# Where the modulation pieces of the second layer are computed: in the FFNs, or all of them inside the Even mixer

## The chip, the cores and the metric

One core of one Trainium2 chip runs the whole program. The metric is the device time of one execution in microseconds; less is better. Engines are named as the profile names them: PE is TensorE's matmul stream, PEld its weight loads, DVE is VectorE, ACT is ScalarE, POOL is GpSimd, SP is SyncE, which here only issues DMAs.

## What is computed

Two trunk layers over 640 tokens, 128 of context and 512 latent ones, with 1024 features. A layer is a half-step FFN, a mixer and a second half-step FFN, each between a modulated norm and a gated norm. The mixer of the first layer (Even) is a gated DeltaNet beside a latent attention (MLA); that of the second (Odd) is a gated linear attention. The nine modulation vectors of a layer come from one small product per layer:

```python
def adaln(cond, w, b):
    m = (jax.nn.silu(cond) @ w + b).reshape(cond.shape[0], 1, N_MOD, D_MODEL)
    return [m[:, :, j] for j in range(N_MOD)]
...
for i in range(DEPTH):
    m_ctx = adaln(c_ctx[None, :], mod_w[i], mod_b[i])
    m_lat = adaln(c, mod_w[i], mod_b[i])
    xc = ffn_branch(xc, m_ctx[0:3], ...)
    ...
    yc, s_ctx = odd_mixer(hc, *w, s0)
    ...
    xs = xs + m_lat[5] * rmsnorm(ys, norm_post[i, 1])
```

`mod_w[i]` is 1024 x 9216, so its bytes are many and its rows of `cond` are two (context and latent). The product depends on nothing else that the layers compute and may be done at any time before its use.

## The kernel before

The order of the work is that of the layers: first FFN, Even mixer, second FFN (both of layer 0), third FFN, Odd mixer, fourth FFN (layer 1). All matmuls of the layers are made of three products of high and low parts (L208 the projections, L650 the up matmuls of the FFNs, L298 the down and out projections). An FFN is a loop over column tiles of L650, with L298 for two token groups (384 and 256 tokens).

**The modulation.** `adaln` (L364 to L421) is a generator. Each step of it is a piece: one of eight row blocks (128 rows) of one of five column groups of a layer; groups 0 to 3 have 2048 columns, group 4 has 1024. There are 80 pieces. A piece loads two tiles `mw` of 512 KB (one in group 4) on SP's queue (L376), into the pool of load buffers of which there are seven, which the weights of the FFNs and of the out projection use too. While the Even mixer's code runs (`look` is true) the next piece's load is issued one piece ahead. At each second piece the matmuls L395 of the pair are issued: for either row block one product per column tile of 512 columns, four tiles (two in group 4), with the 32 columns of `cT` as the stationary side; the four column tiles lie side by side in the array (`tile_position`) and accumulate in one PSUM bank `ad`, of which there is one. The profile shows each such product as two records, so a pair is 16 records, 8 in group 4. After the last row block a bias tile `mb`, taken from the load buffers as well, is loaded on ACT's queue, added by DVE (L403), for groups 0 to 3 turned by four transposes on PE (L407) into a bank of the PSUM pool `pt`, and copied out (L413), or multiplied and written as gates (L415 to L420). In the mixer the banks of `pt` are held by its ring of work banks (`misc`), until the mixer's end.

**Who asks for pieces.** Whoever calls the filler: eight pieces before the first FFN; the FFNs, `FILLS[layer][n]` = (pieces in the loop, pieces at its tail); the Even mixer with `self.fill(n)` in its projections, its heads, its MLA heads (`MFILL`) and beside; the Odd mixer with a flush. The first FFN takes 22, so pieces 1 to 30 are out when the mixer starts. The mixer asks for 31, up to piece 61, the second FFN for 16, and the third for the three left.

**The Even mixer's gated DeltaNet.** Its four heads and two directions are worked as two pairs of heads. For a pair come, in this order: `gdn_prep` (L1164; the decay matrices of five chunks: transposes and products on PE, then DVE and ACT), `gdn_inverse` (L1191; DVE alone, row by row), `gdn_levels` (L1226; two levels of products L1232, L1236 and transposes L1239 on PE with copies on ACT and DVE between them, then a last one), and `gdn_chain`, which walks the state through `gdn_step` (L1259) in five steps. The second pair's work and the MLA's (L1488 to L1584) are written so that one lies beside the other.

**What sets the order.** A tile scheduler orders each engine's instructions when the program is built: by the order of the code, raised for marked parts, and by what is ready and which buffers are free. The engines then run their rows strictly in that order.

Of the kernel before, what the change touches and what calls it, by code (L numbers as in the profile page):

```python
# [27 lines left out]
HW = (6400, 4096)  # L28
HT = TOK // 2
PLAIN = 2  # L30
FILLS = (((16, 6), (10, 6)), ((18, 0), (0, 0)))
EARLY = 5
SLOTS = ((2, 3, 4, 5, 6), (0, 1, 2, 3, 4))
TW = 648
# [858 lines left out]
class Even(Mixer):  # L893
# [87 lines left out]
    def run(self, nxt):  # L981
# [184 lines left out]
        def gdn_prep(pair, st, misc, ering):  # L1166
            for c in range(NT):
                cs = slice(c * P, (c + 1) * P)
                pb, pk, E = misc(), misc(), ering()
                for u, d, h in units(pair):  # L1170
                    nc.tensor.transpose(un(pb, u), gc[:, d, c, h:h + 1].to_broadcast([P, P]), T.ident)
                for h2 in range(2):
                    kc = k[2 * pair + h2][:, cs]
                    nc.tensor.matmul(un(pk, 2 * h2), lhsT=kc, rhs=kc, start=True, stop=True)
                    nc.tensor.matmul(un(pk, 2 * h2 + 1), lhsT=kc, rhs=q[2 * pair + h2][:, cs], start=True, stop=True)
                for u, d, h in units(pair):
                    nc.vector.scalar_tensor_tensor(un(E, u), un(pb, u), gc[:, d, c, h:h + 1], neg[d], ALU.subtract, ALU.min)
                nc.scalar.activation(E[:, :512], E[:, :512], AF.Exp)
                pair_view = lambda t, h2: t[:, h2 * 256:h2 * 256 + 256].rearrange("p (d t) -> p d t", d=2)
                if c:  # L1180
                    Qe = st.Q[c]
                    nc.scalar.activation(Qe, pb, AF.Exp)
                    for h2 in range(2):
                        w = pair_view(Qe, h2)
                        nc.vector.tensor_mul(w, w, q[2 * pair + h2][:, cs].unsqueeze(1).to_broadcast([P, 2, P]))
                for h2 in range(2):
                    nc.vector.tensor_mul(pair_view(st.att[c], h2), pair_view(E, h2), un(pk, 2 * h2 + 1).unsqueeze(1).to_broadcast([P, 2, P]))
                for u, d, h in units(pair):
                    nc.vector.scalar_tensor_tensor(un(st.A[c], u), un(pk, 2 * (u // 2)), nbp[:, c, d * 4 + h:d * 4 + h + 1], un(E, u), ALU.mult, ALU.mult)
# [35 lines left out]
        def gdn_levels(st):  # L1225
            for lv in (4, 5):  # L1226
                mask = T.cm[:, lv].unsqueeze(1).to_broadcast([P, 4, P])
                for c in range(NT):
                    a, uu, dd = st.A[c], st.U[c], st.D[c]
                    py, pz = misc(), misc()  # L1230
                    for u in range(4):
                        nc.tensor.matmul(un(py, u), lhsT=un(a, u), rhs=un(dd, u), start=True, stop=True)  # L1232
                    Y = ering()
                    nc.scalar.copy(Y[:, :512], py)
                    for u in range(4):
                        nc.tensor.matmul(un(pz, u), lhsT=un(Y, u), rhs=un(uu, u), start=True, stop=True)  # L1236
                    nc.vector.copy_predicated(v4(uu), mask, v4(pz))
                    for u in range(4):
                        nc.tensor.transpose(un(py, u), un(uu, u), T.ident)  # L1239
                    nc.scalar.copy(dd, py)  # L1240

            lo, hi = slice(0, 64), slice(64, 128)
            where = ((hi, lo), (lo, hi))
            for c in range(NT):
                a, uu, dd = st.A[c], st.U[c], st.D[c]
                py, pz, Y = misc(), misc(), ering()
                for u in range(4):
                    r, k = where[u % 2]
                    nc.tensor.matmul(un(py, u)[r, k], lhsT=un(a, u)[:, r], rhs=un(dd, u)[:, k], start=True, stop=True, tile_position=(0, r.start))
                by = lambda t, d: t[:, :512].rearrange("p (h d t) -> p h d t", h=2, d=2)[:, :, d]  # L1250
                for d, (r, k) in enumerate(where):
                    nc.scalar.copy(by(Y, d)[r, :, k], by(py, d)[r, :, k])
                for u in range(4):
                    r, k = where[u % 2]
                    nc.tensor.matmul(un(pz, u)[k, r], lhsT=un(Y, u)[:, k], rhs=un(uu, u)[:, r], start=True, stop=True, tile_position=(0, k.start))
                for d, (r, k) in enumerate(where):
                    nc.vector.tensor_copy(by(uu, d)[k, :, r], by(pz, d)[k, :, r])

        def gdn_step(pair, st, work, S, cu, last, ctx):  # L1259

            at = lambda c: slice(c * P, (c + 1) * P)
            if not last:
                pt, kdt = misc(), work()
# [23 lines left out]
            for u, d, h in units(pair):  # L1287
                c = cu[d]
# [10 lines left out]
        def gdn_chain(pair, st):  # L1299
# [19 lines left out]
            def context():  # L1319
                po = gdn_step(pair, st, work, S0, (0, 0), False, True)  # L1320
                for u, d, h in units(pair):
                    nc.scalar.dma_start(self.outs["new_gdn_state"][0, 0, d, h], un(S0, u))
                    od = oT[h][:, 0:P]
                    if d == 0:
                        nc.scalar.copy(od, un(po, u))
                    else:
                        nc.vector.tensor_add(od, od, un(po, u))
                        square(h, 0)
# [64 lines left out]
        self.mark = T.tc.tile_snap_priority()  # L1393
        st0 = gdn_store(0)
        gdn_prep(0, st0, misc, ering)
        gdn_inverse(0, st0, ering)
        for b in range(4):
# [26 lines left out]
        def mla_keys():  # L1424
# [41 lines left out]
            nc.scalar.dma_start(self.outs["new_mla_ckv"][0, 0], nck)  # L1466
        mla_keys()
        gdn_levels(st0)
        gdn_chain(0, st0)
        st1 = gdn_store(1)  # L1470
        e1 = Ring([T.W(name="E") for _ in range(2)])
        gdn_prep(1, st1, mb, e1)


# [134 lines left out]
        gdn_inverse(1, st1, ering)  # L1609
        early = [gdn_out(0)]  # L1610
        gdn_levels(st1)
        self.fill(2)
        gdn_chain(1, st1)
# [417 lines left out]
def trunk_kernel(tc, i, cst, outs):  # L2031
    nc = tc.nc
    with ExitStack() as ctx:
# [11 lines left out]
        for l in range(2):  # L2045
            for n in range(3):
                a = (mods(l, n), gates(l, n), step)
                if n != 1:
                    subs.append(Ffn(T, i["ffn_w_in"][l, n // 2], i["ffn_w_out"][l, n // 2], *a, FILLS[l][n // 2]))
                elif l == 0:  # L2050
# [41 lines left out]
```

## Time and profile before

| | |
|---|---|
| time, median of 3 runs | 2714.06 us (2709.87 to 2714.55) |
| profiled execution | 2716.26 us, span 2714.5 us |
| PE busy | 2632.5 us, 97% of the span, 16040 records |
| PEld busy | 2331.2 us, 86% |
| DVE busy | 1943.0 us, 72% |
| ACT busy | 1179.1 us, 43% |
| POOL busy | 125.5 us, 5% |
| read from and written to memory | 286.59 MB and 20.33 MB |

The span is what lies between the first and the last instruction of the profiled execution. Busy times of an engine are the union of its records; matmuls overlap, so a record may be longer than the time to the next one. In the views by stage, PEclk is the granted TensorE clock as a share of full speed. In a timeline a row is a group of records of one line, its first number the start of the first of them, and in brackets stands the idle time ahead of it and what ended it.

### The profile page before, as it was taken

The numbers are of one execution on the slowest core, as the hardware profiler recorded it, in microseconds if no ns is written. First come the engines' busy times: TensorE is split into PE (matmuls) and PEld (weight loads), VectorE is DVE, ScalarE is ACT, GpSimd is POOL, SyncE is SP. The second block draws the span as 40 slices with busy tenths as digits, with TensorE's granted clock in tenths as the row PEclk, the third lists the DMA queues.
The fourth block names the chain that finished last, engine by engine and source line by source line (L and its number), as shares of the span: only waits on it lengthen the run. The fifth ranks groups of instructions, "written<-read, shape, count | busy, mean of one in ns | idle before, by whom it ended". The sixth has DMA issues, their size and how long they took to land. (4 is left out here: it accounts for less than half of the span.)

```text
span 2714.5 us, 41232 instructions
## 1 busy us (share of the span) xinstructions
PE 2632.5 (97%) x16040; PEld 2331.2 (86%) x16040; DVE 1943.0 (72%) x3731; ACT 1179.1 (43%) x2281; POOL 125.5 (5%) x301
## 2 busy tenths in 40 slices
PE   6999999999999999999999999999999999999998
PEld 4988888789858678888997999999899988999997
DVE  5777777768585558777778777777675749777776
ACT  5433333554345645332335433334765447333333
POOL 0000000200100010000001000000200002000001
PEclk8999999999999999999999999999999999999999
DMA  8334424734151334343227322224212143332222
GB/s 272 123 115 141 148 96 133 251 103 142 50 188 46 128 117 130 114 138 103 86 71 244 104 87 86 86 81 135 92 55 67 59 140 109 95 92 86 78 70 101
DMA packets 297099, 309.60 MB, mean 114 GB/s; under 512 B 13573, under 2 KB 250639, under 8 KB 296903
## 3 DMA queue, kind: packets, MB, share of 16 engines
q1 hardware_dynamic: 278240, 260.05, 30.1%
q10 hardware_dynamic: 18663, 46.92, 4.9%
q8 instruction: 126, 2.06, 0.3%
q14 instruction: 70, 0.57, 0.1%
HBM read 286.59 MB, written 20.33 MB: 113 GB/s over the span
## 5 line engine op out<-in xcount | busy, mean ns | idle before, releaser
L650 PE MATMUL up<-ar,hi 128*128 128x320 f32 x2944 | 658.6, 311 | 10.5 <-ACT ar L513 4.5
L650 PEld LDWEIGHTS up<-ar,hi 128*128 128x128 f32 x2944 | 502.4, 189 | 37.2 <-ACT ar L513 6.1
L650 PE MATMUL up<-ar,lo 128*128 128x320 f32 x1472 | 455.5, 310 | 0.6 <-DVE lo L604 0.6
L603 ACT CAST hi<-raw 128x1024 fp32r<-128x1024 f32 x256 | 268.1, 1050 | 295.4 <-PE up L650 258.4
L304 DVE TENSOR_TENSOR y<-y,dn 128x512 f32<-128x512 f32 x388 | 264.5, 682 | 151.9 <-PE dn L298 150.8
L604 DVE TENSOR_TENSOR lo<-raw,hi 128x1024 fp32r<-128x1024 f32 x256 | 312.4, 1222 | 75.1 <-ACT hi L603 74.5
L298 PE MATMUL dn<-hi,al 128*128 128x512 f32 x880 | 347.8, 395 | 0.1
L298 PE MATMUL dn<-lo,ah 128*128 128x512 f32 x880 | 347.6, 395 | 0.0
L298 PE MATMUL dn<-hi,ah 128*128 128x512 f32 x880 | 346.8, 395 | 0.7 <-DVE y L304 0.5
L650 PE MATMUL up<-hq,hi 128*128 128x320 f32 x1408 | 315.1, 310 | 0.3 <-DVE xn L707 0.3
L650 PEld LDWEIGHTS up<-ar,lo 128*128 128x128 f32 x1472 | 277.9, 189 | 1.3 <-DVE lo L604 1.3
L208 PE MATMUL up<-ar,hi 128*128 128x384 f32 (+1 forms) x1184 | 267.3, 315 | 4.9 <-ACT ar L274 4.0
L650 PEld LDWEIGHTS up<-hq,hi 128*128 128x128 f32 x1408 | 238.8, 188 | 21.5 <-issue 9.2
L650 PE MATMUL up<-hq,lo 128*128 128x320 f32 x704 | 217.4, 309 | 0.0
L208 PEld LDWEIGHTS up<-ar,hi 128*128 128x128 f32 x1184 | 200.6, 191 | 15.3 <-issue 5.6
L183 DVE TENSOR_TENSOR lo<-raw,hi 128x1024 fp32r<-128x1024 f32 x145 | 175.8, 1218 | 45.0 <-ACT hi L182 38.2
L298 PEld LDWEIGHTS dn<-hi,al 128*128 128x128 f32 x880 | 165.3, 188 | 39.3 <-DVE al L691 1.2
L298 PEld LDWEIGHTS dn<-hi,ah 128*128 128x128 f32 x880 | 165.2, 188 | 26.3 <-DVE y L304 1.4
L208 PE MATMUL up<-ar,lo 128*128 128x384 f32 (+1 forms) x592 | 184.3, 311 | 0.0
L298 PEld LDWEIGHTS dn<-lo,ah 128*128 128x128 f32 x880 | 165.1, 188 | 22.2
L182 ACT CAST hi<-raw 128x1024 fp32r<-128x1024 f32 x145 | 150.9, 1048 | 44.5 <-PE up L208 19.0
L658 ACT COPY h<-up 128x320 f32<-128x320 f32 x68 | 29.0, 426 | 314.3 <-PE up L650 314.3
(704 smaller groups left out, 4216.2 us busy)
## 6 DMA issues: line engine op xcount, KB each, us to landing
raw<-in_ffn_w_in_dram SPq DMA_DIRECT2D x188, 512.0 KB
mw<-in_mod_w_dram SPq DMA_DIRECT2D x144, 512.0 KB
raw<-in_ffn_w_out_dram SPq DMA_DIRECT2D x88, 512.0 KB
xdr<-x ACTq DMA_DIRECT2D x25, 512.0 KB
x<-xdr ACTq DMA_DIRECT2D x25, 512.0 KB
raw<-in_od_w_in_dram SPq DMA_DIRECT2D x24, 512.0 KB
raw<-in_ev_w_in_dram SPq DMA_DIRECT2D x19, 512.0 KB
gb<-gate ACTq DMA_DIRECT2D x12, 512.0 KB
```

Of the source, the lines that this page charges most:

```text
L182: nc.scalar.copy(hi, raw)
L183: nc.vector.tensor_sub(lo, raw, hi.bitcast(F32))
L208: self.nc.tensor.matmul(ps[:, :n], lhsT=wt[a][:, kc], rhs=self.h[g][:, b, kc], start=k == 0, stop=k == 3 * KC - 1)
L298: nc.tensor.matmul(ps, lhsT=a(i, m), rhs=w[j][:, nh * 512:nh * 512 + 512], start=k == 0, stop=k == last)
L304: nc.vector.tensor_add(yd, yd, ps)
L603: nc.scalar.copy(hi, raw[:, :n])
L604: nc.vector.tensor_sub(lo, raw[:, :n], hi.bitcast(F32))
L650: nc.tensor.matmul(ps[:, :HT], lhsT=w[i][:, kc], rhs=b[j].at(kc), start=first and n == 0, stop=n == 11, skip_group_check=not first)
L658: self.T.nc.scalar.copy(p1, X[:, :HT])
```

## The change

The second and third FFN ask for no pieces any more. In their place the Even mixer asks for up to 23 more: one in each of the five chunks of the second pair's `gdn_prep`, one at each odd chunk of the two levels of `gdn_levels` (four a call, two calls), and one at the start of each `gdn_step` (five a chain, two chains). The mixer now asks for more than the 50 pieces that are left, and the last of them is given out before its end.

```diff
@@ -28,7 +28,7 @@
 HW = (6400, 4096)
 HT = TOK // 2
 PLAIN = 2
-FILLS = (((16, 6), (10, 6)), ((18, 0), (0, 0)))
+FILLS = (((16, 6), (0, 0)), ((0, 0), (0, 0)))
 EARLY = 5
 SLOTS = ((2, 3, 4, 5, 6), (0, 1, 2, 3, 4))
 TW = 648
@@ -1167,6 +1167,8 @@
             for c in range(NT):
                 cs = slice(c * P, (c + 1) * P)
                 pb, pk, E = misc(), misc(), ering()
+                if pair:
+                    self.fill(1)
                 for u, d, h in units(pair):
                     nc.tensor.transpose(un(pb, u), gc[:, d, c, h:h + 1].to_broadcast([P, P]), T.ident)
                 for h2 in range(2):
@@ -1228,6 +1230,8 @@
                 for c in range(NT):
                     a, uu, dd = st.A[c], st.U[c], st.D[c]
                     py, pz = misc(), misc()
+                    if c % 2:
+                        self.fill(1)
                     for u in range(4):
                         nc.tensor.matmul(un(py, u), lhsT=un(a, u), rhs=un(dd, u), start=True, stop=True)
                     Y = ering()
@@ -1258,6 +1262,7 @@
 
         def gdn_step(pair, st, work, S, cu, last, ctx):
 
+            self.fill(1)
             at = lambda c: slice(c * P, (c + 1) * P)
             if not last:
                 pt, kdt = misc(), work()
```

The line numbers of the code behind the second and third hunk shift: L1232, L1236 and L1239 of before are L1236, L1240 and L1243 in the changed kernel, and the MLA's lines are five higher.

Three places of PE's order show what moves. In these rows `ad` is the pieces' PSUM bank, `mw` their weight tile (a number for each), `x2` two products alike.

The first place is the end of the second FFN (L298, its down projection; L257, the transposes of the next norm) and the start of the third (L650). Before:

```order
6066 L298 MATMUL dn_13681<-lo_13272,ah_13247 128x512
6067 L298 MATMUL dn_13681<-hi_13271,al_13248 128x512
6068 L257 MATMUL pt_13622<-ident,xn_13603 128x128 x4
6069 L395 MATMUL ad_10645<-mw_13695,cT 32x512
6070 L395 MATMUL ad_10645<-mw_13697,cT 32x512 x2
6071 L650 MATMUL up_13862<-ar_13346,hi_13495 128x320
6072 L650 MATMUL up_13888<-ar_13346,hi_13501 128x320
6073 L650 MATMUL up_13862<-ar_13346,hi_13495 128x320
6074 L650 MATMUL up_13862<-ar_13346,lo_13496 128x320
6075 L407 MATMUL pt_13710<-ident,mb_13707 128x128 x4
6076 L395 MATMUL ad_13719<-mw_13720,cT 32x512 x2
```

After:

```order
6088 L298 MATMUL dn_13745<-lo_13336,ah_13311 128x512
6089 L257 MATMUL pt_13669<-ident,xn_13667 128x128 x4
6090 L298 MATMUL dn_13745<-hi_13335,al_13312 128x512
6091 L257 MATMUL pt_13686<-ident,xn_13667 128x128 x4
6092 L650 MATMUL up_13883<-ar_13410,hi_13559 128x320
6093 L650 MATMUL up_13909<-ar_13410,hi_13565 128x320
6094 L650 MATMUL up_13883<-ar_13410,hi_13559 128x320
```

The pieces' products and the transposes of the bias tile (L407) are gone from here, and the up matmuls follow the transposes directly.

The second place is in `gdn_levels` of the second pair (`ar` and `E` are its matrices, `pt` and `dn` the work banks). Before:

```order
3286 L1236 MATMUL dn_4818<-ar_7144,E_5415 128x128 x4
3287 L1236 MATMUL pt_4820<-ar_7144,E_5416 128x128 x4
3288 L1532 MATMUL up_6648<-ckv_6424,ukv_7259 128x384
3289 L1239 MATMUL pt_4821<-ident,ar_7144 128x128 x4
3290 L1532 MATMUL up_6646<-ckv_6424,ukv_7259 128x384
3291 L1239 MATMUL dn_4819<-ident,ar_7144 128x128 x4
3292 L1232 MATMUL pt_4821<-ar_7145,ar_7144 128x128 x4
3293 L1232 MATMUL dn_4819<-ar_7145,ar_7144 128x128 x4
3294 L1236 MATMUL dn_4818<-ar_7144,E_5415 128x128 x4
```

After:

```order
3317 L395 MATMUL ad_7900<-mw_8026,cT 32x512
3318 L1236 MATMUL pt_4821<-ar_7226,ar_7225 128x128 x4
3319 L1236 MATMUL dn_4819<-ar_7226,ar_7225 128x128 x4
3320 L395 MATMUL ad_7900<-mw_8026,cT 32x512
3321 L395 MATMUL ad_7900<-mw_8028,cT 32x512 x2
3322 L395 MATMUL ad_7900<-mw_8128,cT 32x512
3323 L1240 MATMUL dn_4818<-ar_7225,E_5415 128x128 x4
3324 L1240 MATMUL pt_4820<-ar_7225,E_5416 128x128 x4
3325 L1243 MATMUL pt_4821<-ident,ar_7225 128x128 x4
3326 L395 MATMUL ad_7900<-mw_8128,cT 32x512
3327 L395 MATMUL ad_7900<-mw_8130,cT 32x512 x2
```

Two groups of four matmuls used to follow each other, or one of the MLA's stood between them; now products of the pieces do, one to four at a time. Over the whole mixer the products of the second layer's pieces stand in 29 runs before, 80 products in all, and in 54 runs after, 136 products.

The third place is the mixer's end (L298 the out projection, the others the last MLA head). Before:

```order
3635 L1575 MATMUL dn_4818<-ident,pr_8481 128x128
3636 L298 MATMUL dn_8881<-ar_8203,oh_7728 128x512 x2
3637 L407 MATMUL pt_7479<-ident,mb_7476 128x128 x4
3638 L407 MATMUL pt_8374<-ident,mb_8371 128x128 x4
3639 L1579 MATMUL up_6646<-V_7261,cq_6425 128x128
3640 L1579 MATMUL up_6646<-V_7262,cq_6425 128x128 x2
```

After:

```order
3675 L1580 MATMUL dn_4818<-ident,pr_8656 128x128
3676 L298 MATMUL dn_9036<-ar_8414,oh_7869 128x512 x2
3677 L407 MATMUL pt_7011<-ident,mb_7008 128x128 x4
3678 L407 MATMUL pt_7361<-ident,mb_7358 128x128 x4
3679 L1584 MATMUL up_6646<-V_7400,cq_6425 128x128
3680 L1584 MATMUL up_6646<-V_7401,cq_6425 128x128
3681 L407 MATMUL pt_7687<-ident,mb_7684 128x128 x4
3682 L1584 MATMUL up_6646<-V_7401,cq_6425 128x128
3683 L407 MATMUL pt_8210<-ident,mb_8207 128x128 x4
```

Before, the transposes of two finished column groups stand here; now those of all four do.

## Rows read from the trace of the kernel before

**Rows 1.** Page, section 1: busy us, share of the span, instructions of each engine.

```profile
PE 2632.5 (97%) x16040; PEld 2331.2 (86%) x16040; DVE 1943.0 (72%) x3731; ACT 1179.1 (43%) x2281; POOL 125.5 (5%) x301
```

**Rows 2.** Table by stage, the second, third and fourth FFN: us, each engine's busy us (instructions), PEclk, DMA share, GB/s.

```profile
1015.60:1442.10 426.50, 421.46 (x2531) 386.24 (x2532) 323.59 (x504) 163.31 (x257) 8.72 (x15) 1.00 0.36 114
1470.90:1892.40 421.50, 420.41 (x2492) 385.22 (x2492) 319.67 (x507) 161.28 (x256) 9.16 (x21) 1.00 0.33 102
2269.00:2683.00 414.00, 409.86 (x2457) 382.33 (x2456) 317.01 (x496) 159.99 (x251) 6.69 (x12) 1.00 0.29 89
```

**Rows 3.** Table by stage, the mixer in four stretches: the inverse's, and the sum.

```profile
745.00:820.00 75.00, 71.74 (x445) 45.91 (x446) 62.17 (x290) 37.27 (x122) 2.71 (x3) 1.00 0.52 189
...
sum 275.00, PE 267.47 PEld 202.45 DVE 174.11 ACT 139.11 POOL 15.71; mean PE 66.87 PEld 50.61 DVE 43.53 ACT 34.78 POOL 3.93
```

**Rows 4.** Waits of PE, 685 to 960 us (total, times, longest): first and last of eleven.

```profile
PE up L1457 <- POOL ro L235: 1.9, 1, 1.9
...
PE dn L1236 <- ACT E L1234: 0.2, 1, 0.2
```

**Rows 5.** Timeline of PE, second FFN (start, us, line, operation, records).

```profile
1112.22 1.92 PE L395 MATMUL ad<-mw,cT 128*32 128x512 f32 x16
1114.08 0.56 PE L650 MATMUL up<-hq,hi 128*128 128x320 f32 x2
```

**Rows 6.** Timeline of PE, Even mixer.

```profile
738.81 1.07 PE L395 MATMUL ad<-mw,cT 128*32 128x512 f32 x8
739.81 0.49 PE L1271 MATMUL pt<-g,kq 128*128 128x128 f32 x2
740.23 1.04 PE L395 MATMUL ad<-mw,cT 128*32 128x512 f32 x2
741.20 0.49 PE L1271 MATMUL pt<-g,kq 128*128 128x128 f32 x2
```

**Rows 7.** Groups of PE by line: L395 in 1000 to 1600, then in 685 to 960.

```profile
L395 PE MATMUL ad<-mw,cT 128*32 128x512 f32 x112 | 20.8, 632 | 0.0
...
L395 PE MATMUL ad<-mw,cT 128*32 128x512 f32 x160 | 31.5, 604 | 0.0
```

**Rows 8.** Table by stage, the first 200 records of L650 in each FFN.

```profile
1015.60:1053.70 38.10, 32.15 (x200) 30.86 (x201) 0.96 0.42 125
1470.90:1509.60 38.70, 30.56 (x200) 29.42 (x201) 0.96 0.52 171
2269.00:2304.60 35.60, 30.57 (x200) 29.33 (x200) 1.00 0.38 119
```

**Rows 9.** Timeline of PE, from the second FFN to the third.

```profile
1458.23 1.90 PE L395 MATMUL ad<-mw,cT 128*32 128x512 f32 x10
1460.06 0.50 PE L298 MATMUL dn<-hi,ah 128*128 128x512 f32 x1
...
1467.60 1.06 PE L395 MATMUL ad<-mw,cT 128*32 128x512 f32 x6
1470.94 0.81 PE L650 MATMUL up<-ar,hi 128*128 128x320 f32 x3 [2.29 <-ACT ar L513]
...
1472.02 0.63 PE L407 MATMUL pt<-ident,mb 128*128 128x128 f32 x4
1472.58 5.32 PE L395 MATMUL ad<-mw,cT 128*32 128x512 f32 x16
1477.83 0.56 PE L650 MATMUL up<-ar,hi 128*128 128x320 f32 x2
```

**Rows 10.** Table by stage, a stretch of that place.

```profile
1473.00:1476.40 3.40, 3.40 (x10) 0.76 (x8) 3.40 (x10) 0.81 (x3) 0.00 (x0) 0.50 0.64 191
```

**Rows 11.** Transfers of 685 to 960 us: GB/s in 40 slices.

```profile
GB/s 0 2 5 86 116 0 2 38 259 310 22 261 244 4 173 285 304 127 184 76 60 0 2 0 40 0 4 38 248 49 405 8 0 2 229 271 114 77 137 245
```

**Rows 12.** Timeline of PE, the mixer's end.

```profile
948.90 1.05 PE L407 MATMUL pt<-ident,mb 128*128 128x128 f32 x8
```

**Rows 13.** Waits of SP's queue, 685 to 960 us (total, times, longest).

```profile
SPq L376 <- PE ad L395: 135.7, 17, 29.0
```

## The prediction, made before the changed kernel ran

> **What bounds the kernel now.** The page's busy times come first: TensorE (PE) is busy 97% of the span, VectorE 72%, ScalarE 43% [rows 1]. So the first question of any moved work is what PE pays for it at its new place. The table by stage comes second. The second, third and fourth FFN run the same matmuls, and only the fourth holds no modulation piece: 426.50, 421.50 and 414.00 us, with PE busy to within 5.0, 1.1 and 4.1 us of the whole [rows 2]. The stretch of the Even mixer that takes the moved pieces, 685 to 960 us, is 275.00 us long with PE busy 267.47, so PE stands still there for 7.5 us in all; even under the long VectorE inverse (745 to 820 us, VectorE busy 62.17 of 75) it is 3.3 us [rows 3]. The view of waits confirms it: the longest in that stretch is 1.9 us, the shortest of eleven 0.2 [rows 4]. Both the place that gives and the place that takes are full.
>
> **What a piece costs.** L395 is one 512-column product per row block and column tile. Two runs of it are found in the timeline. In the FFN a whole pair of row blocks (16 records) goes in one run: from 1112.22 to the next matmul at 1114.08, 1.86 us [rows 5]. In the mixer the scheduler cuts the pairs: a run of 8 records takes 738.81 to 739.81, 1.00 us; a run of 2 takes 740.23 to 741.20, 0.97 [rows 6]. The price is thus per run, not per record: the column tiles of one run go side by side, and a run with only one of them lasts as long as one with four. I take 0.98, between these two, for a run in which no column tile comes twice, 1.86 where one does.
>
> **Term 1, what leaves the FFNs.** 112 records move out, the others (160) are in the mixer already [rows 7]. In pairs that is the last of column group 2, four of group 3 and four half-wide ones of group 4.
> - Second FFN: it is 12.5 us longer than the fourth [rows 2]. Its first 200 up matmuls take 38.10 us against 35.60 [rows 8], and no piece runs in them, so 2.5 of it stay. Returned: 10.0. (Its four runs at 1.86 and one set of L407 at 0.56 [rows 9] make only 8.0, the lower bound.)
> - Third FFN: 7.5 longer [rows 2], all of it with pieces in it: a run of 16 takes 5.25 us, from 1472.58 to 1477.83 [rows 9], since PE had stood still for 2.29 us just before and then ran 3.40 us at a granted clock of 0.50, which is 1.2 of 2.4 GHz [rows 10]. I count all 7.5. If the wait stays and other matmuls run at the half clock instead, half of 3.4 is kept and 5.8 come back.
> - Between the two, a run of 10 records at 1458.23, 1.83 us [rows 9], returned. The run of 6 at 1467.60 lies ahead of the 2.29 us wait for ScalarE and covers part of it: returned 0, and 1.06 at most, if the wait doesn't grow.
> Sum 19.3, between 15.6 (8.0 + 5.8 + 1.8) and 22.9 (12.5 + 7.5 + 1.83 + 1.06).
>
> **Term 2, what the mixer pays.** The order of PE's rows is fixed when the program is built, so the runs can be counted ahead. Before, the pieces of the second layer in the mixer make 29 runs, 28 of 0.98 and one of 1.86: 29.3 us. After, they make 54, of which 51 at 0.98, two at 1.86 and one (ten products in a row, so one tile thrice) at 2.74: 56.4 us. That is 27.1 more for nine more pairs, which uncut would cost 16.7 (9 x 1.86; a half-wide pair has two column tiles and still two products in each). The cuts are seen in the second order shown above: in the second pair's levels one to four products of a pair stand between two groups of four matmuls. Two more L407 sets, 0.56 each, come to the mixer's end: 1.1. Against it stand PE's idle 7.5 us. The runs are put ahead of whatever the scheduler has ready, mostly not at the waits (which hang on VectorE and ScalarE and move along with PE's delay), so I let them absorb 2. Sum +26.2. Bounds: 10.3 (uncut and all 7.5 absorbed: 16.7 + 1.1 - 7.5), and 35.7 (nothing absorbed, and the waits twice as long because the inverse starts later and the same attention matmuls have to cover it: 27.1 + 1.1 + 7.5).
>
> **What costs nothing.** The moved loads (28 tiles of 512 KB at most) and bias loads are the same bytes, earlier. In the mixer more than a third of the slices show under 25 GB/s [rows 11], so there is room; what happens if the buffers run out is a rival below. VectorE does two more L403 adds and their copies there, while it is busy 174 of 275 us [rows 3]; PE, not VectorE, sets that pace outside the inverse. On SP's queue the loads of the attention weights, of the out projection and of the second FFN now stand behind more piece loads; none of PE's eleven waits hangs on a load now, so I take nothing for it, and the doubled waits above hold its bound. ScalarE gets two bias loads: under 1 us of queue time.
>
> **Sum.** -19.3 + 26.2 = +6.9. On the profiled execution, 2716.26 us, that is 2723.2; this execution is 2.2 above the median of the three runs shown, 2714.06, so I forecast **2721**. The least a measurement of this kernel can tell from no change is about 0.2%, 5.4 us. The bounds of both terms together give -12.6 (10.3 - 22.9) to +20.1 (35.7 - 15.6), that is 2701 to 2734.
>
> **Rival 1: cutting costs only the switch.** If the column tiles of different runs do not lose their overlap (a short run's tail lies under the neighbouring matmuls), a cut costs what two runs of 8 cost over one of 16: 2 x 1.00 - 1.86 = 0.14 us [rows 5, 6]. Then the mixer pays 16.7 + 25 x 0.14 + 1.1 - 2 = 19.3, and the time is 2714, no change. Against it: the run of 2 records kept PE for 0.97, with a plain transpose right behind it [rows 6]. Chance 0.20. The Trainium skill has a rule of this kind: TensorEngine Tiling (Array Packing), under Key Properties, says that a change of the tiling mode drains the engine, so by it alone every extra run has the same small price; the row of the short run speaks for the larger one.
>
> **Rival 2, the other sign: the new places are free.** The new steps stand where the chain of the state and the inverse leave PE waiting for VectorE and ScalarE. If the pieces go in uncut and take all of the 7.5 us, the mixer pays the lower bound, 10.3, and the time is 2714 - 9.0 = 2705. It becomes faster by more than the measurement's 5.4 once the mixer pays under 13.9, that is when over half of the 28.2 is hidden; the view shows 7.5 us to hide it in [rows 3, 4]. What speaks for it: a busy PE is not PE at its peak, and waits of a few tenths may lie inside the matmuls' modelled ends. Chance 0.12. Here too a page bears on it: the Trainium skill, Perfetto Trace Analysis, Identifying the Most-Contended Engine, calls matmul busy time a poor measure and would read the weight loads instead, which are busy 202.45 of the 275 us [rows 3]; by that, there would be 72 us of room and the pieces would be free, 2695. The runs in the timeline, each of which moves the next matmul by its whole length [rows 6], do not bear that out.
>
> **Rival 3: the load buffers run out.** A finished column group keeps its bias tile in one of the seven load buffers until its L407 has run, and L407 waits for the mixer's last steps: the L407 of both groups that end in the mixer now runs at 948.90, close to its end [rows 12]. After the change four groups end there (the third order above), so the last eight pairs load through four and then three buffers, and SP already waits 135.7 us for pieces to free them [rows 13]. If PE, which works strictly in order, meets at each of these eight pairs a tile that is not there, it pays one tile's transfer each time: 512 KB at 310 GB/s [rows 11], 1.7 us, an estimate. 8 x 1.7 = 13.6 more: 2734. For it: order and buffers. Against: each piece's load is issued one piece ahead. Chance 0.18.
>
> That the change does not do what it says can be left out: in PE's order the last piece stands inside the mixer.
>
> **How the numbers follow.** Forecast 0.50 (2715 to 2727, from halving or doubling what is absorbed and from the ends of term 1), rival 1 0.20, rival 2 0.12, rival 3 0.18. Faster by over 5.4 us (under 2709): nearly all of rival 2 and a little of rival 1, 0.13. Within: the rest of rival 1 and the lower third of the forecast, 0.35. Slower: 0.52. The range 2709 to 2733 leaves out rival 2 and half of rival 3.
>
> **What would show it.** After the change the second and third FFN should take about 416.5 and 414 us and hold no L395; the stretch of the mixer should hold 272 records in 54 runs and be 26 us longer, with PE still busy over 95% of it. A mixer only 17 to 20 longer is rival 1, one 10 to 14 longer with PE's idle time gone is rival 2, and waits of PE at L395 for loads are rival 3. I am wrong in the sign of term 2's surplus if a run of 2 records moves the next matmul by much less than 0.97 us.

## The result, and the profile after

The changed kernel takes 2741.14 us (median of 4 runs, 2737.16 to 2745.10) against 2714.31 before: a ratio of 1.0103, 95% interval 1.0084 to 1.0121. It is slower, as forecast, but by 26.8 us where 6.9 were forecast, and outside the range (2709 to 2733). The profiled execution's span grew from 2714.5 to 2739.0, by 24.5.

The page's first section of the changed kernel, beside [rows 1]:

```profile
PE 2653.9 (97%) x16040; PEld 2337.8 (85%) x16040; DVE 1940.2 (71%) x3731; ACT 1180.2 (43%) x2281; POOL 129.3 (5%) x301
```

TensorE is 21.4 us busier, with the same 16040 records. The table by stage for the second, third and fourth FFN, beside [rows 2]:

```profile
1055.80:1473.20 417.40, 412.40 (x2463) 384.55 (x2464) 318.51 (x498) 163.29 (x257) 8.73 (x15) 1.00 0.32 95
1500.90:1914.80 413.90, 412.33 (x2455) 385.60 (x2456) 315.90 (x496) 161.09 (x258) 12.19 (x21) 0.99 0.30 90
2292.90:2706.90 414.00, 409.86 (x2456) 382.10 (x2455) 317.06 (x496) 160.02 (x251) 6.71 (x12) 1.00 0.30 89
```

The second FFN is 9.1 us shorter and the third 7.6, and all three now take 414 to 417 us. With 1.1 between the two, 17.8 came back: close to the 19.3 of term 1.

The rest is the mixer. From the last up matmul of the first FFN to the first of the second, the table by stage shows before:

```profile
480.90:1015.60 534.70, 518.32 (x3384) 415.10 (x3383) 359.89 (x1072) 270.09 (x677) 45.27 (x119) 0.99 0.37 126
```

and after:

```profile
479.10:1055.80 576.70, 558.36 (x3504) 423.30 (x3503) 364.21 (x1087) 271.10 (x677) 45.41 (x119) 0.98 0.43 144
```

It grew by 42.0 us; TensorE is busy in 40.0 of them, so it waits only some 2 more (16.4 and 18.3). The stretch that answers to 685 to 960 us of before ends at 1000.2 now, 40 us longer, and TensorE is busy in 97% of it. Its table row and its group of L395, which answer to [rows 3] and [rows 7]:

```profile
685.00:1000.20 315.20, 304.96 (x1980) 208.91 (x1979) 177.13 (x628) 138.72 (x383) 15.76 (x18) 0.97 0.43 145
```

```profile
L395 PE MATMUL ad<-mw,cT 128*32 128x512 f32 x272 | 63.3, 607 | 2.5 <-DMA mw<-in_mod_w_dram 1.9 <-DVE mb L403 0.4
```

All 272 records are here, as counted. A run's time, from its start to the next matmul, adds up over the mixer to 79.7 us where it was 50.3: 29.4 more, for 27.1 forecast. Nothing in TensorE's waits takes the place of a bound (engine, line, what it waited for, total, times, longest):

```profile
PE pt L257 <- DVE xn L252: 4.6, 2, 2.8
PE pt L1276 <- DMA g<-in_state_gdn_dram: 2.5, 3, 1.2
PE ad L395 <- DMA mw<-in_mod_w_dram: 2.4, 5, 1.0
```

What the forecast did not have is in the granted clock. In the table by stage, around 951 us:

```profile
947.00:951.00 4.00, 3.17 (x13) 1.81 (x11) 3.60 (x8) 3.28 (x6) 0.00 (x0) 0.97 0.39 137
951.00:964.10 13.10, 13.10 (x37) 8.87 (x37) 5.31 (x23) 4.34 (x15) 0.00 (x0) 0.50 0.08 27
964.10:966.00 1.90, 1.90 (x14) 1.58 (x13) 0.52 (x2) 1.77 (x6) 0.00 (x0) 0.91 0.22 91
```

13.1 us at 1.2 GHz, in which TensorE is busy throughout. The timeline ahead of it (start, length, line, operation, records; in brackets the idle time ahead):

```profile
929.36 1.04 PE L395 MATMUL ad<-mw,cT 128*32 128x512 f32 x2
...
947.81 0.35 PE L1551 MATMUL up<-hq 128*128 128x256 f32 x1 [0.61 <-DVE hq L1506]
...
950.35 0.38 PE L1551 MATMUL pt<-kr,ar 128*128 128x256 f32 x1 [0.17 <-ACT ar L1528]
```

The last piece stands at 929.36; two short idle times of 0.61 and 0.17 us come just before the clock falls, in the scores of the third and fourth MLA head. Before, the same heads had pieces between their scores and kept the full clock, as a row of the timeline and the table by stage around it show:

```profile
917.83 1.06 PE L395 MATMUL ad<-mw,cT 128*32 128x512 f32 x8
...
910.00:942.00 32.00, 31.73 (x188) 22.13 (x186) 17.96 (x59) 19.74 (x56) 0.00 (x0) 1.00 0.37 133
```

### The profile page after: what moved, and what is told of

Its sections match the earlier page's. It is cut to its first block, busy times and chain, and to the rows that moved or that the text cites. A ratio compares the mean times of both kernels' runs of the same rounds, so it can differ in the third digit from the quotient of the medians.

```text
span 2739.0 us, 41272 instructions
## 1 busy us (share of the span) xinstructions
PE 2653.9 (97%) x16040; PEld 2337.8 (85%) x16040; DVE 1940.2 (71%) x3731; ACT 1180.2 (43%) x2281; POOL 129.3 (5%) x301
## 5 line engine op out<-in xcount | busy, mean ns | idle before, releaser
L650 PE MATMUL up<-ar,hi 128*128 128x320 f32 x2944 | 661.3, 312 | 12.1 <-ACT ar L513 5.8
L650 PEld LDWEIGHTS up<-ar,hi 128*128 128x128 f32 x2944 | 504.6, 190 | 36.7 <-ACT ar L513 6.7
L650 PE MATMUL up<-ar,lo 128*128 128x320 f32 x1472 | 456.7, 311 | 0.6 <-DVE lo L604 0.6
L298 PE MATMUL dn<-hi,ah 128*128 128x512 f32 x880 | 347.2, 395 | 1.0 <-DVE y L304 0.8
L298 PE MATMUL dn<-hi,al 128*128 128x512 f32 x880 | 347.9, 395 | 0.0
L298 PE MATMUL dn<-lo,ah 128*128 128x512 f32 x880 | 347.5, 395 | 0.0
L650 PE MATMUL up<-hq,hi 128*128 128x320 f32 x1408 | 314.3, 310 | 1.1 <-DVE xn L707 1.1
L650 PEld LDWEIGHTS up<-ar,lo 128*128 128x128 f32 x1472 | 279.0, 190 | 1.3 <-DVE lo L604 1.3
L650 PEld LDWEIGHTS up<-hq,hi 128*128 128x128 f32 x1408 | 239.1, 188 | 18.2 <-issue 6.7
L650 PE MATMUL up<-hq,lo 128*128 128x320 f32 x704 | 217.2, 309 | 0.0
L298 PEld LDWEIGHTS dn<-hi,al 128*128 128x128 f32 x880 | 165.3, 188 | 39.2 <-DVE al L691 0.9
L298 PEld LDWEIGHTS dn<-hi,ah 128*128 128x128 f32 x880 | 165.2, 188 | 26.6 <-DVE y L304 2.1
L298 PEld LDWEIGHTS dn<-lo,ah 128*128 128x128 f32 x880 | 165.1, 188 | 22.4
```

What stands on the lines that cost most here:

```text
L298: nc.tensor.matmul(ps, lhsT=a(i, m), rhs=w[j][:, nh * 512:nh * 512 + 512], start=k == 0, stop=k == last)
L650: nc.tensor.matmul(ps[:, :HT], lhsT=w[i][:, kc], rhs=b[j].at(kc), start=first and n == 0, stop=n == 11, skip_group_check=not first)
```

## The experiments

Every kernel's mixer (from the first FFN's last up matmul to the second's first) is taken apart in the same way: the time in runs of pieces (from each run's start to the next matmul), TensorE's idle time (length less busy time), and half of the time at a granted clock of 0.50, which is what such a stretch costs work that would go at 1.00. The rest is what is left.

| kernel | time, us | mixer | runs of pieces | idle | half of the time at 0.50 | rest |
|---|---|---|---|---|---|---|
| before | 2714.31 | 534.7 | 50.3 | 16.4 | 3.4 | 464.6 |
| changed | 2741.14 | 576.7 | 79.7 | 18.3 | 10.2 | 468.5 |
| e1 changed again | 2738.61 | 574.7 | 79.4 | 17.7 | 10.2 | 467.4 |
| e2 changed, uncut | 2737.35 | 572.6 | 62.7 | 32.8 | 17.0 | 460.1 |
| e3 before, uncut | 2720.99 | 536.2 | 42.5 | 21.3 | 13.6 | 458.8 |
| e4 without gdn_prep's pieces | 2734.24 | 570.4 | 75.6 | 18.9 | 8.5 | 467.4 |
| e5 bias early | 2734.79 | 579.1 | 80.9 | 18.8 | 11.9 | 467.5 |
| e6 uncut, bias early | 2729.52 | 570.8 | 63.7 | 33.0 | 13.6 | 460.5 |
| e7 gdn_prep first | 2752.64 | 587.4 | 82.2 | 23.0 | 18.7 | 463.5 |
| e8 before, gdn_prep first | 2727.13 | 547.2 | 51.6 | 19.5 | 18.7 | 457.4 |
| e9 before, no pieces in the MLA | 2729.96 | 532.2 | 27.4 | 24.6 | 17.0 | 463.2 |
| e10 before, bias early | 2714.55 | 537.6 | 49.1 | 15.5 | 10.2 | 462.8 |
| e11 gdn_step's pieces only | 2733.44 | 560.4 | 65.8 | 16.1 | 8.5 | 470.0 |
| e12 gdn_levels' pieces only | 2737.29 | 567.9 | 66.4 | 21.9 | 10.2 | 469.4 |
| e13 changed, clock kept | 2741.53 | 577.0 | 78.8 + 7.9 | 16.7 | 5.1 | 468.5 |
| e14 before and 23 products | 2745.26 | 562.5 | 52.6 + 22.5 | 15.3 | 6.8 | 465.3 |

(7.9 and 22.5 are the added products' times, from the timeline.) The rest stays within 457 to 470 us through all sixteen, so the other three columns carry most of the differences between the kernels; of a few microseconds the table can't tell the cause. Half of the time is also somewhat too much where TensorE waits within a stretch, as in e8 (busy 24.01 of 27.3 us).

**e1: the same again.** No edit.

> The changed kernel once more, unaltered, for the stretch in the last MLA heads in which TensorE ran 13.1 us at a granted clock of 0.50 (951 to 964 us), which costs about 6.5 us. Theory A (the clock falls there because the pieces are used up before these heads and nothing keeps TensorE fed through the waits at their start): the stretch is there again, at the same place and about as long; time about 2741 us. Rival (the clock falls by chance in single executions): no such stretch, or one elsewhere, and about 2734 us.

2738.61 us (ratio 1.0096, 1.0081 to 1.0111). The stretch is there again at the same place, 10.2 us long:

```profile
950.50:960.70 10.20, 10.20 (x30) 7.05 (x30) 4.45 (x19) 3.57 (x12) 0.00 (x0) 0.50 0.00 0
```

So it belongs to the kernel and is not an accident of one execution. Its length does vary: half of it is 5.1 us here and 6.8 in the changed kernel's profile, and e1 has another 3.4 us at 0.50 at 745.7.

**e2 and e3: pairs uncut.** In `adaln`, for the changed kernel and for the kernel before:

```diff
-for k, wt, j in [(k, wt, j) for k, wt in held for j in range(nj)] ...:
-    nc.tensor.matmul(..., start=k == 0, stop=k == KC - 1, ...)
...
+todo = [(k, wt, j) for k, wt in held for j in range(nj)] ...
+first, last = (0, KC - 1) if one else (1, KC - 2)
...
+for k, wt, j in todo if one else todo[::-1]:
+    nc.tensor.matmul(..., start=k == first, stop=k == last, ...)
```

> The changed kernel with the products of a pair issued last tile first, so that a pair can begin only when all its tiles are there and one product per column tile always stands together: in TensorE's order 62 runs of pieces in place of 83, by 0.98 us for a run and 0.87 for each further round of column tiles 79.9 us in place of 101.4. Theory (the price is per run): 21 us less, about 2720 us. Rival (a cut costs only the switch, 0.14 us each): 3 us less, about 2738 us. Second rival (the loads or the load buffers set the pace, not the runs): no change, and waits of TensorE for the tiles' loads grow.

> The kernel before with the same edit: 55 runs of pieces in place of 68, by the price per run 80.0 us in place of 92.7. Theory (price per run): 12.7 us less, about 2701 us. Rival (switch only): 2 us less, about 2712 us.

2737.35 (1.0092, 1.0077 to 1.0107) and 2720.99 us (1.0027, 1.0014 to 1.0039): no measurable gain for the one, a loss for the other, where the price per run alone had asked for 2720 and 2701. The mixer's time in runs did fall, by 17.0 and 7.8 us for 21 and 11 runs fewer, which is nearer to the price per run than to the switch's 0.14 each; idle time rose by 14.5 and 4.9 and the half clock took 6.8 and 10.2. A pair that begins with its last tile needs its tiles at once and is ready later, and so is the group's end. VectorE's timeline in e2 shows the bias load as the new wait, with the levels' own step queued right behind it:

```profile
869.53 0.69 DVE L406 TENSOR_TENSOR mb<-mb,ad 128x512 f32<-128x512 f32 x1 [8.37 <-DMA mb<-in_mod_b_dram]
870.14 0.72 DVE L1244 COPY_PREDICATED ar<-cm,dn 128x512 f32<-128x512 uint8 x1
```

and TensorE's waits show both, the tiles' loads and the levels' transposes that hang on that step:

```profile
PE ad L398 <- DMA mw<-in_mod_w_dram: 5.4, 6, 2.0
...
PE pt L1246 <- DVE ar L1244: 4.3, 1, 4.3
```

**e5 and e6: the bias early**, at the group's start and into a small buffer of its own, for the changed kernel and for e2:

```diff
+bias = self.S([P, 512], "bias", 1)
+nc.scalar.dma_start(bias[0:rows], ...)
...
-nc.scalar.dma_start(mb[0:rows, 0:512], ...)
-nc.vector.tensor_add(mb[0:rows, 0:512], mb[0:rows, 0:512], ps[0:rows, :])
+nc.vector.tensor_add(mb[0:rows, 0:512], bias[0:rows], ps[0:rows, :])
```

> The changed kernel with each column group's bias loaded at the group's start into a small buffer of its own; the load buffer is taken only when the sum is written. Theory C (TensorE's runs of pieces set the mixer's length) and theory D (the chain of the second pair's gdn_prep, inverse and levels sets it) both expect no change, 2737 to 2743 us, since VectorE waits for the bias under 2 us in the changed kernel. Rival (the bias loads and the load buffers hold the mixer up): 5 us less or more than that.

> Pairs uncut as in e2, and the bias early as in e5: takes away the 16.5 us that VectorE waited for bias loads in e2, where TensorE's time in runs had fallen by 17 us and its idle time had risen by 14.5. Theory C (price per run; e2 lost it to waits that its own edit brought): idle time of TensorE in the mixer falls from 33 to about 20 us and the time to about 2725. Theory D (the chain of the second pair sets the mixer's length, whatever TensorE's sum): levels of the second pair start near 838 us as in e2, time 2733 or more.

2734.79 (1.0080, 1.0065 to 1.0095) and 2729.52 us (1.0055, 1.0040 to 1.0070). In e5 the mixer gained nothing, 579.1 us; the few microseconds lie in the first FFN (429.5 us, 434.5 in the changed kernel). In e6 the first FFN gains the same 5 to 6, and the mixer only 1.8 against e2. Its idle time stayed at 33.0, where theory C had asked for 20, though the wait for the bias is gone; TensorE's longest waits are now spread over tile loads and several other causes, of which these are the first:

```profile
PE ad L400 <- DMA mw<-in_mod_w_dram: 7.3, 4, 4.4
PE pt L257 <- DVE xn L252: 4.6, 2, 2.8
PE pt L1362 <- DVE kq L1322: 3.4, 2, 2.5
```

So the mixer of the uncut kernel is held by waits that changed their names. Which one would be last is not settled.

**e4: without the pieces in gdn_prep.** The two lines of the diff's second hunk are left out.

> The changed kernel without the five steps in the second pair's gdn_prep: all pieces but the last pair at most still lie in the Even mixer, and they last into the third MLA head. Runs 81 in place of 83, 98.5 us of them in place of 101.4. Theory A (the clock falls where the pieces have run out): no stretch at half clock in the mixer's MLA heads, 3 us for the runs and 6.5 for the clock less, about 2731 us. Rival (the clock falls for another reason at the start of the third head, whatever the pieces do): the half clock stays, about 2738 us.

2734.24 us (1.0079, 1.0064 to 1.0094), between the two. No stretch near 951, as theory A said. But idle times of 1.3 to 2.0 us at three other places had stretches of 3.4 to 6.8 us behind them, so that the half clock cost 8.5 in place of 10.2: theory A was right on the place and wrong on the gain.

**e7 and e8: gdn_prep first.** For the changed kernel and for the kernel before:

```diff
+here = T.tc.tile_snap_priority()
 gdn_levels(st0)
 gdn_chain(0, st0)
...
-gdn_prep(1, st1, mb, e1)
+with T.ahead(T.tc.tile_snap_priority() - here):
+    gdn_prep(1, st1, mb, e1)
```

> The changed kernel with the second pair's gdn_prep given the priority of the first pair's levels, so that pieces no longer take the places that it had there before: its products stand at rows 3008 to 3059 of TensorE's order, in the changed kernel up to row 3180. The pieces make 86 runs in place of 83, 104.3 us in place of 101.4. Theory C: 3 us more, about 2742 us. Theory D (the change's price is that gdn_prep, and with it inverse and levels of the second pair, come 20 to 27 us later): the levels start near 822 us in place of 844, and the time is 10 us or more less, 2730 or under.

> The kernel before with the same priority for the second pair's gdn_prep, which there stands early already. 67 runs of pieces in place of 68, 90.9 us in place of 92.7. Theories C and D: 0 to 2 us less. If it is slower by over 3 us, the place of gdn_prep has a price of its own and e7 has to be read against that.

2752.64 (1.0138, 1.0121 to 1.0155) and 2727.13 us (1.0052, 1.0037 to 1.0067): both slower than the kernels that they were made from. The levels of the second pair did begin early in e7, at 820 us in place of 844, and the mixer was longer all the same: theory D falls as it was put on record. The run is no clean test of it, though: the last of the levels' products L1236 stands at 874.5 us, in the changed kernel at 871.3, so the chain began earlier and did not end earlier. e8 shows what the move costs by itself, and if that price adds up in e7 too, the early start gained 1.8 us of mixer (10.7 us longer in e7, 12.5 in e8) and not 10. e8's mixer is 12.5 us longer, and the half clock takes 15.3 more, nearly all in one stretch in the first MLA head, in which no piece stands:

```profile
796.60:823.90 27.30, 24.01 (x73) 16.84 (x73) 15.14 (x57) 13.26 (x45) 0.00 (x0) 0.50 0.05 18
```

**e9: no pieces in the MLA heads**, on the kernel before:

```diff
-MFILL = ((1, 1, 1, 1, 1, 1, 0), (1, 1, 1, 1, 1, 1, 0), (1, 0, 1, 0, 1, 0, 0), (0, 0, 0, 0, 0, 0, 0))
+MFILL = ((0, 0, 0, 0, 0, 0, 0),) * 4
```

> The kernel before without pieces in the MLA heads: 15 pieces fewer in the mixer, taken by the second and third FFN, whose loops ask for as many as are left. In all 56 runs of pieces, 85.3 us, in place of 68 and 92.7. Theory A (TensorE keeps its full clock through the MLA heads only while pieces stand between their products): stretches of 10 us and more at a granted clock of 0.50 in the MLA heads, where before had none; 7 us of runs less, 7 to 17 us of clock more: 2714 to 2724 us. Rival (pieces and clock have nothing to do with each other): no long stretch, about 2707 us.

2729.96 us (1.0065, 1.0049 to 1.0081): more than either expected. The stretch that theory A asked for is there, after an idle time of 4.07 us:

```profile
783.00:803.50 20.50, 18.04 (x52) 12.62 (x53) 12.78 (x79) 5.26 (x16) 0.00 (x0) 0.50 0.00 0
```

And the mixer is the clearest reading of the series: 22.9 us of runs left it, and it became 2.5 us shorter, because idle time rose by 8.2 and the half clock by 13.6. In the kernel before, the pieces in the MLA heads were nearly free. The third FFN, which took most of those pieces, became 15.1 us longer (436.6 for 421.5). Both expectations had let the mixer give back what its runs took.

**e10: the bias early in the kernel before** (the edit of e5).

> The kernel before with the bias loaded early, as in e5, where the first FFN was 4 to 5 us shorter. 67 runs of pieces, 90.0 us in place of 92.7. If the first FFN gains the same 5 us here and nothing is lost in the mixer: about 2707 us, below both kernels. If the gain of e5 was tied to the order of that kernel: no change, 2714 us.

2714.55 us (1.0004, 0.9993 to 1.0014): no change. The first FFN takes 429.1 us (436.4 in the profile of before), but the mixer is 2.9 longer, with one new stretch of 10.2 us at half clock. Its end falls together with a piece. The table by stage, before and from the first piece of that head, which starts at 790.30:

```profile
781.40:790.20 8.80, 8.28 (x24) 5.85 (x24) 4.47 (x26) 1.50 (x5) 0.00 (x0) 0.50 0.40 162
790.20:792.00 1.80, 1.80 (x4) 0.28 (x3) 1.80 (x16) 0.94 (x3) 0.00 (x0) 0.61 0.00 0
```

At 791.6, inside that run, the clock is back at 1.00. That the piece brought it back is not shown: e1's stretch of the same length ended with no piece near.

**e11 and e12: single parts of the change.** Only the line in `gdn_step`, and only the two lines in `gdn_levels`, with the FFNs asking as before.

> Of the change only the ten pieces in gdn_step (five for either pair); the FFNs ask as before and take what is left. 78 runs of pieces, 97.3 us, in place of 68 and 92.7. By runs alone 5 us more, about 2718 us. If idle time and clock come on top in proportion to what they were in the changed kernel (its mixer paid 42.0 us, of which runs 29.4): 2720 to 2723 us. If the places in the state's chain are free: 2714 us or less.

> Of the change only the eight pieces in gdn_levels (four for either pair). 78 runs, 99.1 us. By runs alone 6 us more, about 2720 us; with idle time and clock in proportion 2722 to 2726 us. If the levels are the place that hurts (each piece stands between products that wait for one another through ScalarE and VectorE): more than e11 by over 3 us.

2733.44 (1.0070, 1.0056 to 1.0084) and 2737.29 us (1.0087, 1.0073 to 1.0102): both above their ranges. Part of the change costs most of what all of it does. In the mixer e11 pays 25.7 us for 80 records and e12 33.2 for 64. The levels are the worse place, by 3.9 us in time and by 7.5 in the mixer, of which 5.8 are idle time.

**e13: the clock kept.** The changed kernel, with products of a piece's shape at the start of the third MLA head's first four score blocks; their results are overwritten:

```diff
 ps, ks = mb(), slice(o, o + n)
+for x in range(4 if h == 2 and m < 4 and j == 0 else 0):
+    nc.tensor.matmul(ps[32 * x:32 * x + 32, :], lhsT=T.cT[:, 0], rhs=ckv[:, 0:512],
+                     start=True, stop=True, tile_position=(0, 32 * x))
```

> The changed kernel with four extra rounds of a piece-like product (four column tiles, 512 columns, its result overwritten) at the start of the third MLA head's first four score blocks, where no piece is left and TensorE ran 10.2 to 13.7 us at a granted clock of 0.50 in three profiles. They stand in 8 runs, about 8 us of TensorE time, and load nothing. Theory A (without such products between the MLA's, the clock stays low once a short idle time has dropped it): the stretch near 951 us shrinks to 3.4 or 6.8 us or goes, which gives back 3.4 to 6.8 us, so 2740 to 2744 us in all. Rival (the clock there has nothing to do with the pieces): the stretch stays at 10 us or more, time 2747 us.

2741.53 us (1.0111, 1.0094 to 1.0127), as theory A had it. The table by stage at the place of the stretch:

```profile
950.70:964.00 13.30, 13.22 (x61) 7.12 (x59) 6.06 (x24) 4.79 (x17) 0.00 (x0) 1.00 0.12 39
```

and the timeline, with the added products (L1550):

```profile
947.04 1.06 PE L1550 MATMUL up<-ckv,cT 128*32 128x512 f32 x8 [0.52 <-DVE hq L1506]
948.04 0.39 PE L1553 MATMUL up<-hq 128*128 128x256 f32 x1
...
949.01 1.04 PE L1550 MATMUL up<-ckv,cT 128*32 128x512 f32 x2
949.99 0.38 PE L1553 MATMUL pt<-kr,ar 128*128 128x256 f32 x1
950.30 1.04 PE L1550 MATMUL up<-ckv,cT 128*32 128x512 f32 x2
951.27 0.38 PE L1553 MATMUL pt<-kr,ar 64*128 64x256 f32 x1
```

The clock stays at 1.00 through it. The 7.9 us of added runs are paid back (5.1 by the half clock, 1.6 by idle time, 0.9 by the pieces' own runs), so this needless work was free, within the few microseconds by which runs of one kernel differ.

What e13 doesn't show is that the clock must fall where pieces are missing. In e2 the last piece of the mixer stands at 928.60, as early as in the changed kernel, the same head waits 0.72 us at its start, and the table by stage gives the full clock up to 990 us:

```profile
949.24 0.35 PE L1554 MATMUL up<-hq 128*128 128x256 f32 x1 [0.72 <-DVE hq L1509]
...
929.00:990.00 61.00, 59.23 (x343) 43.88 (x340) 34.48 (x118) 37.53 (x102) 0.00 (x0) 1.00 0.24 80
```

The second short wait, 0.17 us in the changed kernel, is missing there. So products like the pieces' took the stretch away, and what sets it off stays open.

**e14: the runs alone.** The kernel before, with one product at each of the change's 23 places, and no loads, buffers or bias:

```diff
+nc.tensor.matmul(py[0:32, :], lhsT=T.cT[:, 0], rhs=uu[:, :512],
+                 start=True, stop=True, tile_position=(0, 0))
```

in `gdn_levels` at each odd chunk, and likewise into `pb` in the second pair's `gdn_prep` and into `pv` in `gdn_step` (there ahead of `pv`'s own products, a little later than the change's place).

> The kernel before, its FFN pieces where they are, with one product of a piece's shape (one column tile, 512 columns, its result overwritten) at each of the 23 places of the change: 21 runs more on TensorE, no loads, no buffers, no bias. Theory C (what the change pays in the mixer is TensorE's time for short runs and what that drags in, clock and idle time): 21 runs at 0.98 are 20.6 us, and with the same share on top as in e11 (25.7 for 15.5 us of runs) up to 34: 2734 to 2747 us. Rival (the loads, the load buffers and the bias set the price, and a run alone fits into the waits of the state's chain and the inverse): under 2725 us.

2745.26 us (1.0120, 1.0103 to 1.0137), in theory C's range. The timeline of one of them in the second pair's levels:

```profile
846.80 1.16 PE L1240 MATMUL pt<-ar,E 128*128 128x128 f32 x8
847.89 1.04 PE L1234 MATMUL pt<-ar,cT 128*32 128x512 f32 x2
848.86 0.33 PE L1243 MATMUL dn<-ident,ar 128*128 128x128 f32 x1
```

0.97 us from its start to the next matmul; all 23 add up to 22.5, and the mixer is 27.8 us longer. Nothing of them was hidden in the state's chain or the inverse.

## Why the prediction was wrong, step by step

- **Sign and mechanism** held: the FFNs give back little, the mixer takes more, and it does so because one product costs what four side by side cost. e14 shows this price with nothing else changed.
- **Term 1** held: 17.8 returned for 19.3 forecast, within its bounds. One reading under it was off: the 5.25 us of [rows 9] were put down to the half clock, which is worth only 1.7 of them (half of 3.40); that run holds two half-wide pairs, so either of its column tiles comes four times. Nothing hung on it, since 7.5 was read from the whole stage.
- **Term 2 failed: 42.0 us for 26.2, beyond even its upper bound of 35.7.** Its parts: runs 29.4 for 27.1, a small miss; absorbed idle time, for which 2 were taken off, came out as 1.9 more, so "I let them absorb 2" failed by 3.9. The step that failed most is one that was not there: "Against it stand PE's idle 7.5 us" looks at idle time alone, and no term was given to the clock. The half clock takes 6.8 more in the mixer, all of it in the stretch near 951. e1 shows that it belongs to the kernel, e13 that it goes when piece-like products stand there; that the pieces used up early had kept the clock up in the last heads fits this, but e2 kept it without them. The remaining 3.9 lie in the rest: 1.1 of them had been forecast, for the two L407 sets, and 2.8 stay open. A surcharge of a tenth of a microsecond beside each run would make them, but e14, with 23 products more than before, has a rest only 0.7 longer. The misses 2.3, 3.9, 6.8 and 2.8 add up to the 15.8; without the clock's 6.8 the mixer would have paid 35.2, just inside the upper bound, so the clock is the largest miss and not the only one.
- The bounds of term 2 failed too, since they doubled waits only. The nearest row for a price of the clock, [rows 10], had been read, and used only for the FFN. One small cost was also read too low: two bias loads, put at under 1 us of ScalarE's queue, take 0.57 us each there in the kernel before (median of ten), which changes nothing here.
- **Rival 1** (a cut costs the switch alone, 0.14 us) fell: 0.97 for each product in e14. The Trainium skill's rule on which it leant (TensorEngine Tiling (Array Packing), Key Properties: a change of tiling mode drains the engine) gives no price, and no run here separates such a drain from the 0.97 us.
- **Rival 2** (the places are free) fell by e14 and e11. The Trainium skill's page Perfetto Trace Analysis (Identifying the Most-Contended Engine) would read weight loads, beside the arithmetic done, in place of matmul busy time. Weight loads went from 415.10 to 423.30 us in a mixer that grew by 42.0, so the room that they show was not there for these products.
- **Rival 3** (the load buffers run out) gives nearly the right time, 2734, for the wrong reason. TensorE waits for tile loads 2.4 us in the mixer, not 13.6, and e5, which takes the buffer for the bias later, left the mixer no shorter. In the uncut kernels such waits did appear (5.4 and 7.3 us), as the price of e2's edit.
- The forecast's premise that the mixer was full was only half right. e9 takes 22.9 us of runs out of it and gains 2.5: the pieces in the MLA heads filled waits, or kept the clock up. The added ones cost their full time. e9's pieces and the added ones stand at different places, so whether the place decides or the number already there is not separated. The 7.5 us of idle time in [rows 3, 4] are what was left, not how much the pieces already there hide.

No version beat the kernel before; e10 equals it.

## What to carry to other kernels

An engine that is busy 97% of the time may owe that to filler work that costs nothing where it stands; take some out before adding more, to learn what the stage hides already. Filler can also keep TensorE's clock up (e9, e13): look at the granted clock behind the place where it runs out, before using all of it up early. And price a moved matmul by the time until the next matmul starts at its new place, since four column tiles in one run cost as much there as one alone.

## What the runs showed of the hardware

A needless product can be free. In e13, 7.9 us of extra TensorE work left the time as it was within the noise (2741.53 us, and 2741.14 without), while 13.1 us at 1.2 GHz went back to 2.4.

How long the clock stays low differed much. In MLA heads without pieces stretches at 0.50 were 10.2 us (e1, and e10 up to its first piece), 13.7 (changed, e5), 17.1 (e7), 20.5 (e9) and 27.3 us (e8), with TensorE busy for most or all of them. Elsewhere in the mixer most were 3.4 or 6.8 us. The pieces alone don't decide it: heads without a piece near also had stretches of 3.4 us (816.0 in e12, 821.1 in e11, 806.9 in e9), and one of 10.2 us at 700.4 in e7 has a piece in it. In the changed kernel idle times of 0.61 and 0.17 us stood ahead of its longest stretch, while a single idle time of 1.2 us, at 2207.5 us in the kernel before, brought none.

The clock can also fall with no idle time ahead. In the changed kernel a stretch of 3.4 us begins at 698.2, TensorE has no idle time over 0.1 us in the 16 us before it, and what it ran just before are products of a single column (L1448); the timeline, and the table by stage of the stretch:

```profile
694.27 2.29 PE L1448 MATMUL up<-ones,acc 128*128 128x1 f32 x20
...
698.20:701.60 3.40, 3.40 (x10) 1.54 (x9) 1.86 (x5) 0.59 (x1) 1.77 (x1) 0.50 0.00 0
```
